# The last layer's down projection with held quadrants, and the modulations beside the first one in column groups

## The chip, the cores and the metric

The kernel runs on one core of a Trainium2 chip. A core has a matrix engine (TensorE, PE in the profile), three engines for elementwise work (VectorE or DVE, ScalarE or ACT, GpSimd or POOL), and a queue engine (SyncE or SP) from which nearly all transfers (DMAs) of this kernel are issued. The engines run side by side, each through its own list of instructions in order, and wait for one another on semaphores. Memory on the core is SBUF (128 partitions) and PSUM, which matmuls write. The metric is the time of one execution on the device, in microseconds; lower is better. Times are the median of several executions; the profile is of one more.

## The reference

One inference step of a two-layer trunk of width 1024 for 1152 tokens: 1024 of a prompt and 8 x 16 of samples. Layer 0 mixes over time with a recurrence (RWKV-7), layer 1 with attention over a band; each is followed by a feed-forward part. All is in float32.

```python
mod = jax.nn.silu(c) @ p['w_ada'][l] + p['b_ada'][l]
sh_m, sc_m, gt_m, sh_f, sc_f, gt_f = jnp.split(mod, 6, axis=-1)
...
x = x + gt_m[:, None, :] * out
h = modulate(rms_norm(x, p['norm_ffn'][l]), sh_f, sc_f)
x = x + gt_f[:, None, :] * swiglu(h, p['w_gate'][l], p['w_up'][l], p['w_down'][l])
```

`c` has one row for the prompt and one for each of the 8 samples, 9 in all; so the *modulations* are a product of 9 rows by a 1024 x 14336 matrix (6144 columns for each layer and 2048 for the shared keys and values). The *down projection* is the product with `w_down`, 2816 x 1024, and the gated addition to x after it.

## The kernel before

**Products.** Feature-major: features lie on partitions, tokens along the free dimension. A float32 operand is split into two parts of a narrower format, hi (ScalarE copies, L276) and lo (VectorE subtracts, L277), and each product is three matmuls, hi x hi, hi x lo and lo x hi (`mm3`). All matmuls go through the helper `mm`, so their line is L143. Tokens are in two groups c: the first with 512, the second with 640.

**The down projection** (`down`, for both layers) takes a Strassen scheme: the output is cut into quadrants (h: upper or lower half of the features, t: first or second half of the tokens of a group), and seven products, the *turns* i = 0, 1, 2, 4, 5, 6, 3, make the four. A turn loads its operand from DRAM in three pieces j per group (`operand`, "h<-bd", L1491) and splits them. For each of four output tiles m of 128 features it loads and splits weights (`weights`, "rq<-ws" or "rq<-in_wd", L1502), runs 11 blocks x 3 matmuls for each group into one PSUM tile ("S" or "PT"), and then evicts (L1555) or adds the result to the accumulator (L1536). One output tile is 66 matmuls, one down projection 28 tiles, 1848 matmuls. In layer 0 the last two turns run once for each group alone. When a quadrant is whole, `result` loads x ("xin<-x", L1529), does the gated addition (`residual`, L1174 to L1179), stores (L1531) and in layer 0 squares the rows for the next norm ("kk", "sqa").

Operands, their raw loads and the accumulator all come from one pool for each group, tag h0 or h1, with 14 slots. The accumulator has four slots for each group (`feats`), held from the first turn to the last; one operand in use has six, hi and lo for three pieces.

**The modulations** are computed in a generator that other loops advance (`step`). Units 12 to 27 of 28 run beside layer 0's down projection, three steps after each output tile (L1570). A unit is 512 outputs. A step loads two tiles of 128 x 512 from `wada` ("aw<-in_wada", L264) and runs four matmuls. Each has 32 stationary columns, the rows of silu(c), and writes its own quarter of PSUM's partitions; the four *column groups* take four different blocks of the contraction. Two steps sum one half of a unit's outputs, so that after four steps (8 blocks) the bank "acc" holds, for each output, four partial sums on four groups of partitions. ScalarE copies the 128 x 512 bank out (L226), and four matmuls with a constant of 16 columns ("acc<-cst,aw") transpose it and sum the quarters; VectorE adds the bias (L232). In the profile a float32 matmul has two records. The aw tiles come from a pool of 11 buffers (tag e) that also serves xin, kk and sqa.

**Order.** The program is traced in Python order, and a planner places each instruction by a simulated time: what is ready first goes first, earlier traced work ahead. So the steps of the modulations end up between matmuls of the products where the planner thinks that their data has come. What it emits is fixed; on the chip each engine takes its list in order.

Of the kernel before, what the change touches and what calls it, by code (L numbers as in the profile page):

```python
# [76 lines left out]
def prep(i):  # L77
    i = {k: np.asarray(v) for k, v in i.items()}
    d = {}
    d["cst"] = _CST  # L80
    d["ti"] = _solver_identity()
    t = np.arange(384)
    rs = np.stack([t % 64 != 0, np.where(t < 256, t % 64, t % 16) != 0]).astype(np.float32)
    d["rs"] = np.ascontiguousarray(np.broadcast_to(rs[:, None], (2, 128, 384)))
    x = np.concatenate([i["x_prompt"][0], i["x_sample"].reshape(128, 1024)], 0)
    d["x"] = np.ascontiguousarray(x.reshape(3, 384, 8, 128).transpose(0, 3, 2, 1))

    xp = np.concatenate([np.zeros((1, 1024), np.float32), i["x_prompt"][0]], 0)
    xg = np.concatenate([xp[16 * g:16 * g + 17] for g in range(64)] + [t for s in i["x_sample"] for t in (s[:1], s)], 0)
    d["xg"] = np.ascontiguousarray(xg.reshape(3, 408, 8, 128).transpose(0, 3, 2, 1))  # L90
    c = np.zeros((32, 1024), np.float32)
    c[0:1] = i["c_prompt"]
    c[1:9] = i["c_sample"]
    d["c"] = np.ascontiguousarray(c.reshape(32, 8, 128).transpose(2, 1, 0))
    wa = np.concatenate([i["w_ada"][0], i["w_ada"][1], i["kv_ada_w"]], 1)
    d["wada"] = np.ascontiguousarray(wa.reshape(2, 4, 128, 28, 2, 256).transpose(3, 4, 0, 2, 1, 5)).reshape(28, 4, 128, 1024)
    par = {f"mix{m}": i["rw_mix"][0, m] for m in range(6)}
    par.update(w0=i["rw_w0"][0], a0=i["rw_a0"][0], kk=i["rw_kk"][0], ka=i["rw_ka"][0], rk=i["rw_rk"][0].reshape(-1),
               lnw=i["rw_lnw"][0], lnb=i["rw_lnb"][0], nm0=i["norm_mix"][0], nm1=i["norm_mix"][1],
               nf0=i["norm_ffn"][0], nf1=i["norm_ffn"][1], kvn=i["kv_norm"],  # L100
               kn=np.tile(i["k_norm"], 16), qn=np.tile(i["q_norm"][0], 16),
               bada=np.concatenate([i["b_ada"][0], i["b_ada"][1], i["kv_ada_b"]]))
# [43 lines left out]
class Trunk:  # L146
# [54 lines left out]
    def ada_steps(self, units, tag="aux", bufs=1, tile=None, sbt=None):  # L201

        nc = self.nc

        def load(u, i):
            w = (tile or self.rawtile)()
            if not isinstance(w, tuple):
                w = w[:, :1024],
            n = 1024 // len(w)
            for j, t in enumerate(w):  # L210
                self.wload(t, self.a["wada"][u, i][:, j * n:(j + 1) * n])
            return [t[:, o:o + 256] for t in w for o in range(0, n, 256)]
        todo = [(u, i) for u in units for i in range(4)]
        ahead = None
        for u in units:
            ps = self.bank(tag, bufs)
            for i in range(4):
                w = ahead or load(*todo.pop(0))
                ahead = load(*todo.pop(0)) if todo and self.fetch_ahead else None
                c = slice(i // 2 * 256, i // 2 * 256 + 256)  # L220
                for q in range(4):
                    mm(nc, ps[32 * q:32 * q + 32, c], self.scT[:, i % 2 * 4 + q, :], w[q], i % 2 == 0, i % 2 == 1)
                if i < 3:
                    yield
            sb = (sbt or tile or self.rawtile)()[:, :512]
            nc.scalar.activation(sb, ps, AF.Copy)  # L226
            for j in range(4):
                mm(nc, ps[:, j * 16:(j + 1) * 16], sb[:, j * 128:(j + 1) * 128], self.C("qs"), True, True)
            pv = ps[:, 0:64].rearrange("p (j n) -> p j n", n=16)[:, :, 0:9]
            bo = PAR["bada"] + u * 4  # L230
            bv = self.par[:, bo:bo + 4].rearrange("p (j o) -> p j o", o=1).broadcast_to([128, 4, 9])
            nc.vector.tensor_tensor(self.mod[:, u * 4:u * 4 + 4, :], pv, bv, ALU.add)  # L232
            yield

    def gain(self, name, sc):

# [1155 lines left out]
    def ffn(self, l, B, W, part1, xsrc, dst, done):  # L1392
# [7 lines left out]
        for f in range(1, 22):  # L1400
            self.gate_up(spill(f), B, self.strassen_weights(l, f, nc.vector if f == 1 else None), (0, 1))
            for g in range(32 * (f - 1) // 21, 32 * f // 21):
                self.down_sums(l, g)
        return self.down(l, xsrc, dst, done)

    def down_open(self, l):

# [55 lines left out]
            gp.tensor_tensor(q[:, 1], q[:, 1], q[:, 0], ALU.subtract)  # L1463
        nc.sync.dma_start(self.Ws[m][:, :, j * 176:(j + 1) * 176], q)

    def down(self, l, xsrc, dst, done):

        nc = self.nc
        gate = 48 * l + 40
        ks = [(j, k) for j, n in enumerate((4, 4, 3)) for k in range(n)]  # L1470
        width = (256, 320)
        part = (slice(0, 256), slice(256, 576))
        turns = [(i, (0, 1)) for i in (0, 1, 2, 4, 5)]
        if l:
            turns += [(i, (0, 1)) for i in (6, 3)]
            self.ada = iter(())
        else:
            turns += [(i, (c,)) for c in (1, 0) for i in (6, 3)]
            part512 = lambda: self.ev("aw")[:, 0:512]
            self.ada = self.ada_steps(range(12, 28), "acc", 1, lambda: (part512(), part512()), part512)  # L1480
        acc, end = {}, iter(())
        sq = [Ctx(), Ctx()]

# [11 lines left out]

        def weights(i, m):
            src = {0: 0, 1: 1, 3: 3}.get(i)
            src = self.Ws[m][:, {5: 0, 2: 1, 6: 2, 4: 3}[i]] if src is None else self.a[f"wd{l}"][:, src, m * 1408:(m + 1) * 1408]
            W = []
            for o, n in ((0, 512), (512, 512), (1024, 384)):  # L1500
                raw = self.halfraw()[:, :n]
# [20 lines left out]
        def result(h, t, m, cs):  # L1522
            f = 4 * h + m
            x = self.ev("xin")[:, 0:576]
            for c in cs:
# [3 lines left out]
                nc.sync.dma_start(x[:, part[c]], xsrc[:, f, at])  # L1529
                self.residual(192 if c * t else n, f, gate, o, x[:, part[c]], o)  # L1530
                nc.sync.dma_start(dst[:, f, at], o)  # L1531
                if l == 0:
                    squares(c, t, f, o)

        def add(o, a, b):
            nc.vector.tensor_tensor(o, a, b, ALU.add)  # L1536

        for i, cs in turns:
            X = operand(i, cs)
            if i == 0:  # L1540
# [2 lines left out]
            for m in range(4):  # L1543
                W = weights(i, m)
                d = self.wide()[:, 256:832]
                for c in cs:
                    for n, (j, k) in enumerate(ks):
                        s = slice(k * 128, (k + 1) * 128)
                        hi, lo = (X[c][j][h][:, k] for h in range(2))
                        self.mm3(d[:, part[c]], W[j][0][:, s], W[j][1][:, s], hi, lo, n == 0, n == 10)  # L1550
                for c in cs:
                    z = d[:, part[c]]
                    c11, c12, c21, c22 = (out(h, t, m, c) for h in range(2) for t in range(2))
# [13 lines left out]
                        add(c21, z, c21)  # L1567
                if i in (1, 5, 6, 3):
                    result(*{1: (0, 0), 5: (0, 1), 6: (1, 1), 3: (1, 0)}[i], m, cs)
                self.step(3)  # L1570
                for _ in range(2):
                    next(end, None)
            if l == 0 and i == 3:
                for g in (self.ada, end):
                    for _ in g:
                        pass
                end = done(cs[0], acc[cs[0]], sq[cs[0]])
        return end

    def dense(self, x2, x3, close):  # L1580
        nc = self.nc
# [530 lines left out]
```

## Time and profile before

| what | us |
|---|---|
| median of three runs | 3791.01 |
| the three runs | 3791.89, 3791.01, 3785.09 |
| the profiled execution, its own time | 3785.41 |
| its span, first to last instruction | 3783.6 |
| first product matmul to end of last, down projection of layer 0 | 1807.3 to 2132.5 |
| the same of layer 1 | 3518.1 to 3778.9 |

The profile's page begins with the busy time of each engine. Other views group instructions by form, list them in order of time, or sum them over given stretches. An idle time is shown with the one who ended it: "[3.45 <-ACT h L276]" means that the engine stood idle for 3.45 us until ScalarE's instruction of line 276 that writes tile h. "SPq" rows are transfers being issued. PEclk is the share of TensorE's clock that was granted.

### The profile page before, as it was taken

The numbers are of one execution on the slowest core, as the hardware profiler recorded it, in microseconds if no ns is written. First come the engines' busy times: TensorE is split into PE (matmuls) and PEld (weight loads), VectorE is DVE, ScalarE is ACT, GpSimd is POOL, SyncE is SP. The second block draws the span as 40 slices with busy tenths as digits, with TensorE's granted clock in tenths as the row PEclk, the third lists the DMA queues.
The fourth block names the chain that finished last, engine by engine and source line by source line (L and its number), as shares of the span: only waits on it lengthen the run. The fifth ranks groups of instructions, "written<-read, shape, count | busy, mean of one in ns | idle before, by whom it ended". The sixth has DMA issues, their size and how long they took to land.

```text
span 3783.6 us, 74619 instructions
## 1 busy us (share of the span) xinstructions
PE 3457.2 (91%) x29078; PEld 3088.6 (82%) x29078; DVE 2248.3 (59%) x4380; ACT 1667.9 (44%) x3182; POOL 769.7 (20%) x743
## 2 busy tenths in 40 slices
PE   5788989999889799999999899789888899999999
PEld 3677768777667699999888879677667799999999
DVE  4666666765446765555446742666575776555555
ACT  4545546554223533333344452556564433333342
POOL 0000000000011066676100000000000156667100
PEclk9887899889689899999999999899999899999999
DMA  5776676677666434445788322445565334444764
GB/s 209 233 220 166 199 217 190 194 202 211 180 186 201 141 127 142 139 138 160 265 319 294 123 73 93 144 143 160 159 205 172 133 123 148 143 139 142 243 205 138
DMA packets 548579, 664.12 MB, mean 176 GB/s; under 512 B 137056, under 2 KB 409440, under 8 KB 543744
## 3 DMA queue, kind: packets, MB, share of 16 engines
q1 hardware_dynamic: 472912, 560.62, 46.7%
q0 software_dynamic: 22224, 80.36, 7.0%
q10 hardware_dynamic: 53088, 18.36, 2.1%
q8 instruction: 229, 3.75, 0.4%
q14 instruction: 126, 1.03, 0.1%
HBM read 482.63 MB, written 176.53 MB: 174 GB/s over the span
## 4 chain that ended last, share of the span: by engine, by line
PE 65%; DMA 13%; DVE 10%; issue 6%; ACT 4%; SPq 1%; POOL 1%; ACTq 0%; DVEq 0%; POOLq 0%
PE S L143 30%; PE PT L143 14%; PE acc L143 12%; PE st L143 3%; PE O L143 2%; DMA raw<-in_rw_o 1%; DVE h L277 1%; PE G L143 1%; PE PT L1937 1%; PE aux L143 1%; DMA TT<-Z 1%; DVE wlo L277 1%; DMA bt<-in_rel 1%; DMA xin<-x 1%; DMA h<-bd 1%
## 5 line engine op out<-in xcount | busy, mean ns | idle before, releaser
L143 PE MATMUL S<-h,w 128*128 128x256 f32 (+1 forms) x7374 | 1036.6, 299 | 23.9 <-ACT h L276 7.4
L143 PEld LDWEIGHTS S<-h,w 128*128 128x128 f32 x7374 | 1002.4, 191 | 46.2 <-issue 19.1
L276 ACT ACTIVATE w<-rq 128x512 fp32r<-128x512 f32 (+1 forms) x500 | 304.4, 614 | 661.4 <-PE S L143 290.0
L277 DVE TENSOR_TENSOR w<-rq,w 128x512 fp32r<-128x512 f32 (+1 forms) x500 | 384.4, 773 | 286.6 <-ACT w L276 247.9
L143 PE MATMUL PT<-h,w 128*128 128x256 f32 (+1 forms) x3714 | 532.0, 298 | 10.2 <-DVE h L277 3.8
L143 PE MATMUL acc<-mx,whi 128*128 128x384 f32 x1728 | 505.9, 370 | 37.2 <-ACT whi L276 15.4
L143 PEld LDWEIGHTS PT<-h,w 128*128 128x128 f32 x3714 | 506.4, 190 | 20.5 <-issue 7.8
L143 PEld LDWEIGHTS acc<-mx,whi 128*128 128x128 f32 x1728 | 335.5, 203 | 67.9 <-ACT whi L276 20.1
L143 PE MATMUL acc<-mx,wlo 128*128 128x384 f32 x864 | 314.9, 365 | 9.0 <-DVE wlo L277 9.0
L1373 POOL TENSOR_TENSOR t<-t,t 128x576 f32<-128x576 f32 (+1 forms) x132 | 221.9, 1682 | 262.9 <-ACT t L1380 154.0
L277 DVE TENSOR_TENSOR h<-h,h 128x1024 fp32r<-128x1024 f32 (+6 forms) x152 | 169.3, 1125 | 121.2 <-ACT h L276 111.2
L276 ACT ACTIVATE h<-h 128x1024 fp32r<-128x1024 f32 (+6 forms) x152 | 142.8, 950 | 147.8 <-DMA h<-bd 110.0
L143 PEld LDWEIGHTS acc<-mx,wlo 128*128 128x128 f32 x864 | 174.1, 202 | 21.6 <-DVE wlo L277 13.9
L277 DVE TENSOR_TENSOR wlo<-raw,whi 128x1024 fp32r<-128x1024 f32 x114 | 139.0, 1221 | 83.6 <-ACT whi L276 82.7
L276 ACT ACTIVATE whi<-raw 128x1024 fp32r<-128x1024 f32 x114 | 119.6, 1053 | 128.7 <-PE acc L143 61.6
L143 PE MATMUL S<-h,wh 128*128 128x320 f32 (+1 forms) x744 | 148.5, 348 | 12.7 <-DVE h L1685 4.7
L143 PE MATMUL acc<-h,wh 128*128 128x256 f32 (+1 forms) x864 | 137.9, 309 | 18.4 <-ACT wh L276 9.1
L1373 DVE TENSOR_TENSOR t<-S,t 128x576 f32<-128x576 f32 (+1 forms) x117 | 86.6, 740 | 113.9 <-PE S L143 113.9
L143 PEld LDWEIGHTS S<-h,wh 128*128 128x128 f32 x744 | 123.4, 195 | 31.3 <-ACT wh L276 6.3
L143 PEld LDWEIGHTS acc<-h,wh 128*128 128x128 f32 x864 | 121.2, 200 | 27.2 <-ACT wh L276 9.8
L1303 POOL TENSOR_TENSOR h<-h,h 128x256 f32<-128x256 f32 x12 | 11.0, 942 | 569.9 <-DMA vf<-in_wo 569.9
L1767 POOL MEMSET qbd<- 128x128 f32 x1 | 0.2, 204 | 560.8 <-PE S L143 560.8
(455 smaller groups left out, 5625.8 us busy)
## 6 DMA issues: line engine op xcount, KB each, us to landing
aw<-in_wada SPq DMA_DIRECT2D x128, 256.0 KB, 5.3
bd<-t SPq DMA_DIRECT2D x154, 160.0 KB, 1.9
rq<-in_wg SPq DMA_DIRECT2D x88, 256.0 KB, 2.9
rq<-in_wu SPq DMA_DIRECT2D x88, 256.0 KB, 2.6
ws<-in_wd SPq DMA_DIRECT2D x64, 352.0 KB, 3.6
ws<-ws SPq DMA_DIRECT2D x64, 352.0 KB, 3.3
bd<-t SPq DMA_DIRECT2D x152, 128.0 KB, 1.8
rq<-ws SPq DMA_DIRECT2D x72, 256.0 KB, 3.4
```

The lines of the kernel that those rows point to most:

```text
L143: return nc.tensor.matmul(out, lhsT, rhs, start=start, stop=stop)
L276: self.nc.scalar.activation(hi, x, AF.Copy)
L277: self.nc.vector.tensor_tensor(lo, x, hi, ALU.subtract)
L1303: gp.tensor_tensor(out[j], x[j], y[j], op)
L1373: return eng.tensor_tensor(out, x, y, ALU.add)
L1767: nc.gpsimd.memset(self.qbd, 0.0)
L1937: nc.tensor.transpose(pt[:, j * 128:(j + 1) * 128], P[:, j * 128:(j + 1) * 128], self.C("ident"))
```

## The change

Layer 0's `down` keeps its accumulator. The modulations beside it come from a new generator, `ada_groups`. Its unit is 1024 outputs (8 units). Each of the four column groups takes 256 outputs of its own and all eight blocks of the contraction, so that nothing is left to be summed over the groups; the weights are laid out anew for it (`wadb`). Two steps (two blocks k, 8 matmuls) are taken together: the two tiles of the first come from the pool with tag e, those of the second from a pool "ws" with two buffers of its own, which earlier stages used for another purpose. The first matmul of the eight reads the tile loaded last; the others are tied behind it on TensorE (`issue_after`). The next loads are traced right after the eight. Once a unit is whole, ScalarE copies 128 x 256, and at the next call two matmuls with a constant of 36 columns (`qg`) transpose it. The generator is advanced after each 44 matmuls of the products, within an output tile, where before it was advanced three times after each tile.

The last layer has its own `down_last`. Instead of a four-slot accumulator it holds the results of turns 0, 2 and 4 in one slot for each group and turn (`T`). Finished quadrants go to a new buffer o of the pool with tag e, which the residual and the store use; both token groups go through one residual.

```diff
+    d["wadb"] = np.ascontiguousarray(wa[:, 6144:].reshape(8, 128, 8, 1024).transpose(2, 0, 1, 3))
+    d["qg"] = np.ascontiguousarray(np.tile(np.eye(32, 9, dtype=np.float32), (4, 4)) * np.repeat(np.repeat(np.eye(4, dtype=np.float32), 32, 0), 9, 1))
...
+    def ada_groups(self, spare):
...
+        qg = self.ev("aw")[:, 0:36]
+        nc.sync.dma_start(qg, self.a["qg"])
+        ev = lambda: self.ev("aw")[:, 0:512]
+        steps = [(u, k) for u in range(8) for k in range(8)]
+
+        def load(n):
+            W = []
+            for (u, k), new in zip(steps[n:n + 2], (ev, spare)):
+                t = [new() for _ in range(2)]
+                for h in range(2):
+                    nc.sync.dma_start(t[h], self.a["wadb"][u, k][:, 512 * h:512 * h + 512])
+                W.append([x[:, o:o + 256] for x in t for o in (0, 256)])
+            return W
+
+        def close(u, sb):
+            ps = self.bank("acc", 1)
+            for j in range(2):
+                mm(nc, ps[:, j * 36:(j + 1) * 36], sb[:, j * 128:(j + 1) * 128], qg, True, True)
...
+            for j in range(2):
+                pv = ps[:, j * 36:(j + 1) * 36].rearrange("p (g n) -> p g n", n=9)
+                nc.vector.tensor_tensor(view(self.mod[:, o:o + 8, :])[:, :, j], pv, bv[:, :, j], ALU.add)
+
+        W, last = load(0), None
+        for n in range(0, 64, 2):
+            if last:
+                close(*last)
+                last = None
+            if steps[n][1] == 0:
+                ps = self.bank("acc", 1)
+            u, k = steps[n]
+            todo = [(k + j, q, W[j][q]) for j in (1, 0) for q in (3, 2, 1, 0)]
+
+            def product(at, q, w):
+                return mm(nc, ps[32 * q:32 * q + 32, 0:256], self.scT[:, at, :], w, at == 1, at == 6)
+            lead = product(*todo.pop(0))
+            with self.tc.issue_after(lead.ins):
+                for x in todo:
+                    product(*x)
+            if k == 6:
+                last = u, ev()[:, 0:256]
+                nc.scalar.activation(last[1], ps[:, 0:256], AF.Copy)
+            if n < 62:
+                W = load(n + 2)
+            yield
+        close(*last)
...
-        if l:
-            turns += [(i, (0, 1)) for i in (6, 3)]
-            self.ada = iter(())
-        else:
-            turns += [(i, (c,)) for c in (1, 0) for i in (6, 3)]
-            part512 = lambda: self.ev("aw")[:, 0:512]
-            self.ada = self.ada_steps(range(12, 28), "acc", 1, lambda: (part512(), part512()), part512)
+        turns += [(i, (c,)) for c in (1, 0) for i in (6, 3)]
+        spare = lambda: self.wq.tile([128, 4, 176], F32, tag="ws", name=self.nm("ws"), bufs=2).rearrange("p a b -> p (a b)")[:, 0:512]
+        self.ada = self.ada_groups(spare)
...
                         self.mm3(d[:, part[c]], W[j][0][:, s], W[j][1][:, s], hi, lo, n == 0, n == 10)
+                        count += 3
+                        if count >= 44:
+                            count -= 44
+                            self.step()
...
-                self.step(3)
...
+    def down_last(self, gate, xsrc, dst):
...
+        def hold(n):
+            T[n] = [self.slot(c)[:, :4 * (256, 320)[c]].rearrange("p (m t) -> p m t", m=4) for c in range(2)]
+
+        def result(h, t, m, o):
...
+            x = self.ev("xin")[:, 0:576]
+            for c in range(2):
+                nc.sync.dma_start(x[:, part[c]], xsrc[:, f, at[c]])
+            self.residual(448 if t else 576, f, gate, o, x, o)
+            for c in range(2):
+                nc.sync.dma_start(dst[:, f, at[c]], o[:, part[c]])
+
+        for i in (0, 1, 2, 4, 5, 6, 3):
+            X = operand(i)
+            if i in (0, 2, 4):
+                hold(i)
...
+                o = None if i in (0, 2, 4) else self.ev("o")[:, 0:576]
...
+                if i in (0, 2, 4):
+                    for c in range(2):
+                        nc.scalar.activation(t[i][c], z[c], AF.Copy)
+                oc = None if o is None else [o[:, part[c]] for c in range(2)]
+                if i == 1:
+                    add(oc, z, t[0])
+                    result(0, 0, m, o)
+                elif i == 4:
+                    add(t[2], t[2], t[4])
+                elif i == 5:
+                    add(t[0], z, t[0])
+                    add(oc, t[2], t[0])
+                    result(0, 1, m, o)
+                elif i == 6:
+                    add(t[0], z, t[0])
+                    add(oc, t[4], t[0])
+                    result(1, 1, m, o)
+                elif i == 3:
+                    add(oc, z, t[0])
+                    result(1, 0, m, o)
```

What `down_last` leaves out here, the loads of operands and weights and the matmuls, is as in `down`.

More of the change, by code (lines that the diff above doesn't have):

```diff
@@ L233, in ada_steps @@
             yield
+    def ada_groups(self, spare):
+        nc = self.nc
+        qg = self.ev("aw")[:, 0:36]
[14 more added lines that the diff above has]
+                mm(nc, ps[:, j * 36:(j + 1) * 36], sb[:, j * 128:(j + 1) * 128], qg, True, True)
+            o = 48 + u * 8
+            bo = PAR["bada"] + o
+            view = lambda t: t.rearrange("p (g j) n -> p g j n", j=2)
+            bv = view(self.par[:, bo:bo + 8].rearrange("p (f o) -> p f o", o=1).broadcast_to([128, 8, 9]))
+            for j in range(2):
[23 more added lines that the diff above has]
+        close(*last)
     def gain(self, name, sc):
@@ L1403, in ffn @@
                 self.down_sums(l, g)
-        return self.down(l, xsrc, dst, done)
+        if l:
+            return self.down_last(48 * l + 40, xsrc, dst)
+        return self.down(48 * l + 40, xsrc, dst, done)
     def down_open(self, l):
@@ L1464, in down_sums, with down @@
         nc.sync.dma_start(self.Ws[m][:, :, j * 176:(j + 1) * 176], q)
-    def down(self, l, xsrc, dst, done):
+    def down(self, gate, xsrc, dst, done):
         nc = self.nc
-        gate = 48 * l + 40
         ks = [(j, k) for j, n in enumerate((4, 4, 3)) for k in range(n)]
@@ L1497, in weights @@
             src = {0: 0, 1: 1, 3: 3}.get(i)
-            src = self.Ws[m][:, {5: 0, 2: 1, 6: 2, 4: 3}[i]] if src is None else self.a[f"wd{l}"][:, src, m * 1408:(m + 1) * 1408]
+            src = self.Ws[m][:, {5: 0, 2: 1, 6: 2, 4: 3}[i]] if src is None else self.a["wd0"][:, src, m * 1408:(m + 1) * 1408]
             W = []
@@ L1531, in result @@
                 nc.sync.dma_start(dst[:, f, at], o)
-                if l == 0:
-                    squares(c, t, f, o)
+                squares(c, t, f, o)
         def add(o, a, b):
             nc.vector.tensor_tensor(o, a, b, ALU.add)
+        count = 0
         for i, cs in turns:
@@ L1569, in down @@
                     result(*{1: (0, 0), 5: (0, 1), 6: (1, 1), 3: (1, 0)}[i], m, cs)
-                self.step(3)
                 for _ in range(2):
                     next(end, None)
-            if l == 0 and i == 3:
+            if i == 3:
                 for g in (self.ada, end):
@@ L1578, in down, with operand, weights, add @@
         return end
+    def down_last(self, gate, xsrc, dst):
+        nc = self.nc
+        ks = [(j, k) for j, n in enumerate((4, 4, 3)) for k in range(n)]
+        part = (slice(0, 256), slice(256, 576))
+        T = {}
+        def operand(i):
+            X = {0: [], 1: []}
+            for c in range(2):
+                n = (256, 320)[c]
+                for j, nk in enumerate((4, 4, 3)):
+                    raw, hi, lo = (self.slot(c, dt)[:, :nk * n].rearrange("p (k t) -> p k t", k=nk) for dt in (F32, F32R, F32R))
+                    nc.sync.dma_start(raw, self.Bd[c][i][j])
+                    self.split(hi, lo, raw)
+                    X[c].append((hi, lo))
+            return X
+        def weights(i, m):
+            src = {0: 0, 1: 1, 3: 3}.get(i)
+            src = self.Ws[m][:, {5: 0, 2: 1, 6: 2, 4: 3}[i]] if src is None else self.a["wd1"][:, src, m * 1408:(m + 1) * 1408]
+            W = []
+            for o, n in ((0, 512), (512, 512), (1024, 384)):
+                raw = self.halfraw()[:, :n]
+                nc.sync.dma_start(raw, src[:, o:o + n])
+                W.append([self.wq.tile([128, 512], F32R, tag="w", name=self.nm("w"), bufs=self.hw[2]) for _ in range(2)])
+                self.split(W[-1][0][:, :n], W[-1][1][:, :n], raw)
+            return W
+        def hold(n):
+            T[n] = [self.slot(c)[:, :4 * (256, 320)[c]].rearrange("p (m t) -> p m t", m=4) for c in range(2)]
+        def result(h, t, m, o):
+            f = 4 * h + m
+            at = [slice(512 * c + (256, 320)[c] * t, 512 * c + (256, 320)[c] * (t + 1)) for c in range(2)]
+            x = self.ev("xin")[:, 0:576]
[8 more added lines that the diff above has]
+                hold(i)
+            for m in range(4):
+                W = weights(i, m)
+                d = self.wide()[:, 256:832]
+                for c in range(2):
+                    for n, (j, k) in enumerate(ks):
+                        s = slice(k * 128, (k + 1) * 128)
+                        hi, lo = (X[c][j][h][:, k] for h in range(2))
+                        self.mm3(d[:, part[c]], W[j][0][:, s], W[j][1][:, s], hi, lo, n == 0, n == 10)
+                z = [d[:, part[c]] for c in range(2)]
+                t = {n: [T[n][c][:, m] for c in range(2)] for n in T}
+                o = None if i in (0, 2, 4) else self.ev("o")[:, 0:576]
+                def add(out, a, b):
+                    for c in range(2):
+                        nc.vector.tensor_tensor(out[c], a[c], b[c], ALU.add)
+                if i in (0, 2, 4):
+                    for c in range(2):
+                        nc.scalar.activation(t[i][c], z[c], AF.Copy)
[16 more added lines that the diff above has]
+                    result(1, 0, m, o)
```

## The prediction

> **What bounds the kernel now.** I read the page first: whose work fills the span.
>
> ```profile
> span 3783.6 us, 74619 instructions
> PE 3457.2 (91%) x29078; PEld 3088.6 (82%) x29078; DVE 2248.3 (59%) x4380; ACT 1667.9 (44%) x3182; POOL 769.7 (20%) x743
> ```
>
> TensorE is busy 91% of the span, so time can be won in two ways: take work from TensorE, or close its gaps. The change touches two stages, the first layer's down projection (about 1807 to 2133 us) and the last layer's (3518 to the end). The view of busy time by stretch shows what they lack; columns are length, then each engine's busy us and count, granted TensorE clock, DMA share, GB/s.
>
> ```profile
> core 0: us, PE busy (x) PEld busy (x) DVE busy (x) ACT busy (x) POOL busy (x), PEclk, DMA share, GB/s
> 1822.00:2088.00 266.00, 263.18 (x2088) 225.89 (x2088) 126.59 (x223) 103.77 (x169) 0.00 (x0) 1.00 0.85 295
> 2103.50:2110.30 6.80, 5.34 (x19) 4.56 (x20) 3.97 (x9) 2.75 (x6) 0.00 (x0) 0.50 0.64 200
> 3554.40:3557.60 3.20, 0.26 (x2) 0.00 (x0) 0.00 (x0) 0.61 (x1) 0.00 (x0) 1.00 0.97 341
> 3557.60:3564.40 6.80, 5.62 (x24) 5.33 (x25) 5.72 (x7) 6.25 (x10) 0.00 (x0) 0.50 0.78 300
> 3600.00:3612.00 12.00, 8.70 (x52) 8.08 (x53) 5.96 (x7) 3.12 (x3) 0.00 (x0) 0.87 0.86 278
> 3612.00:3779.00 167.00, 166.88 (x1246) 166.62 (x1244) 90.96 (x162) 59.65 (x93) 0.00 (x0) 1.00 0.51 162
> ```
>
> The last row is the pace of undisturbed work: 167.00 / 1246 = 0.134 us for a matmul of the products (half have 256 columns, half 320). In the first layer's stage TensorE has no gaps but carries foreign work; in the last layer's it has gaps, each followed by a stretch at half clock. DMA is at 0.85 in the first and has room in the second.
>
> **First layer: the modulation work.** Grouped by form over 1822 to 2088 us (busy us, mean ns, then idle before it and what ended that):
>
> ```profile
> L143 PE MATMUL acc<-aw,scT 128*32 128x256 f32 x512 | 45.6, 387 | 1.7 <-DMA aw<-in_wada 1.6
> L143 PE MATMUL acc<-cst,aw 128*128 128x16 f32 x128 | 15.4, 252 | 0.0
> ```
>
> Each step is 4 matmuls, 8 records, so 512 records are the 64 steps; the 128 of the second row are the 16 units' 4 transposes. How these stand between the products is seen in the timeline (start, length, engine; the next row's start tells when the products go on):
>
> ```profile
> 1826.68 0.63 PE L143 MATMUL acc<-aw,scT 128*32 128x256 f32 x4
> 1827.23 0.70 PE L143 MATMUL S<-h,w 128*128 128x320 f32 x3
> ...
> 1836.16 1.01 SPq L264 DMA_DIRECT2D aw<-in_wada  x2
> 1837.45 0.96 PE L143 MATMUL acc<-cst,aw 128*128 128x16 f32 x8
> 1838.26 3.38 PE L143 MATMUL S<-h,w 128*128 128x256 f32 x22
> 1841.57 1.07 PE L143 MATMUL acc<-aw,scT 128*32 128x256 f32 x16
> 1842.57 2.32 PE L143 MATMUL S<-h,w 128*128 128x320 f32 x14
> ```
>
> Half a step costs 0.55 us (1826.68 to 1827.23), two steps in one run 1.00, a unit's transposes 0.81. [...] The change has 64 steps again, with matmuls of the same size, but in 32 runs of two whole steps, tied together behind one leading matmul that reads the last tile loaded: 32 x 1.07 = 34.2 us against 45.6, saving **11.4**. Transposes go from 16 groups of four to 8 of two: 16 x 0.81 = 13.0 against 8 x 0.41 = 3.2, saving **9.7**; the cost follows the count, since each is the load of a 128x128 operand, and 36 columns instead of 16 are still few. Evictions fall from 16 to 8 on ScalarE and the bias adds stay 16; neither engine is over half busy here, so I cost both at nothing. Bytes and DMA count stay, plus one small load. PE work saved: **21**.
>
> **The new wait.** Of a run's four 256 KB loads, two go to a pool with room for two tiles, so they can be issued only once the run before has read those tiles. Queued behind the leading matmul on TensorE are all later products, and they wait with it. A run is due each 44 product matmuls, 44 x 0.134 = 5.9 us; the two tiles are read first in a run, which gives back about 0.5, so 6.4 us are there. What is needed is two issues, 1.0 us (the SPq row at 1836.16 above), and the landing, in the answer on the tile these loads fill:
>
> ```profile
> DMA to landing us min/median/max: 2.6/5.3/7.9
> ```
>
> At the median 1.0 + 5.3 = 6.3 us: just hidden. At the minimum nothing waits; if all landed at the maximum, 8.9 - 6.4 = 2.5 us, 32 times, 80 us. Before, deeper buffers held such waits to 1.6 us in all (the group's row above). I take the value by the median, a little over its zero: 0.16 us a run, **5 us**; ends 0 and 80. First layer: 21 - 5 = **16**.
>
> After the modulations one more wait stands here, for the squares of the finished rows:
>
> ```profile
> 2104.96 2.50 PE L143 MATMUL S<-sqa,cst 128*128 128x320 f32 x4 [3.48 <-DVE sqa L1520]
> ```
>
> It hangs on a chain of residual loads that the change leaves alone. With the half-clock stretch (2103.50 to 2110.30 above: 15 of its 19 matmuls are products, 2.0 us at full pace, in 5.3 us of busy time) it is worth 3.5 and at most 3.3 more. I leave it in the time; it may go, since the modulations end sooner.
>
> **Last layer: the gaps.** Timeline rows around the first two changes of operand (turns 0 to 1 and 1 to 2; brackets: idle before, and who ended it):
>
> ```profile
> 3528.83 0.69 ACT L1555 ACTIVATE h<-S 128x256 f32<-128x256 f32 x2
> 3545.70 8.95 PE L143 MATMUL S<-h,w 128*128 128x256 f32 x66
> 3546.40 0.70 ACT L1555 ACTIVATE h<-PT 128x256 f32<-128x256 f32 x2
> 3550.70 0.90 SPq L1491 DMA_DIRECT2D h<-bd  x2
> 3556.99 1.06 ACT L276 ACTIVATE h<-h 128x1024 fp32r<-128x1024 f32 x1 [9.89 <-DMA h<-bd]
> 3558.10 0.58 PE L143 MATMUL S<-h,w 128*128 128x256 f32 x1 [3.45 <-ACT h L276]
> 3559.36 2.72 PE L143 MATMUL S<-h,w 128*128 128x256 f32 x11 [0.68 <-DVE h L277]
> ...
> 3588.14 0.82 DVE L1536 TENSOR_TENSOR h<-S,h 128x256 f32<-128x256 f32 x2 [0.35 <-PE S L143]
> 3588.18 0.90 SPq L1491 DMA_DIRECT2D h<-bd  x2
> ...
> 3602.50 1.58 PE L143 MATMUL PT<-h,w 128*128 128x256 f32 x11 [0.53 <-DVE h L277]
> 3607.68 0.39 PE L143 MATMUL PT<-h,w 128*128 128x256 f32 x1 [2.28 <-ACT h L276]
> 3608.67 3.60 PE L143 MATMUL PT<-h,w 128*128 128x256 f32 x14 [0.49 <-DVE h L277]
> ```
>
> The next operand is loaded too late. In turn 1 its first loads (3588.18) go out with the very add of the third output tile (3588.14) that first writes one more slot of the accumulator; in turn 0 they go out soon after the third eviction (3546.40). I read this as the planner giving out the slots of the pool in the order of first use: a load for the next turn queues behind an accumulator slot not yet written. The change holds one slot for a whole quadrant, first written by the first output tile (3528.83 in this trace), and none in turn 1. So turn 1's loads can go out two products, 2 x 8.9 = 17.8 us, earlier, against 3.45 + 0.68 us of lateness; turn 2's too. Also more slots are free: one to three held of 14, not four. The gaps go: 3.45 + 0.68 + 0.53 + 2.28 + 0.49 = 7.4 us. The half clock goes with them: 3557.60 to 3564.40 does 24 x 0.134 = 3.2 us of work in 6.8, and 0.68 of it is counted already, so 2.9; 3600.00 to 3612.00 does 52 x 0.134 = 7.0 in 12, less gaps of 3.3, so 1.7. Together **12.0**. Weights are late next; they are split over one product ahead, so nothing shows.
>
> [...]
>
> What the last layer's change adds: results go to a fresh buffer of the pool that the residual input x is loaded to, and x's load comes after that buffer's first write. It can no longer run far ahead. Inside the stage the 8.9 us of a product hide a load (a landing of about 4 us):
>
> ```profile
> xin<-x SPq DMA_DIRECT2D x32, 160.0 KB, 4.2
> ...
> 3778.92 0.82 DVE L1536 TENSOR_TENSOR h<-S,h 128x256 f32<-128x256 f32 x2 [7.12 <-PE S L143]
> ```
>
> Queued behind the residual on VectorE are weight splits, a product ahead. At the end nothing hides it: between 0 and 4.2 us are added, less the adds' 0.82. The store before it on SP's queue lets it out during the last product, so I take the low side, **1**. Two residuals merged into one save VectorE time that bounds nothing. Last layer: 12 - 1 = **11**.
>
> **Sum.** 16 + 11 = 27 us. The profiled execution took 3785.4 us by its own time (span 3783.6); the three runs have a median of 3791.0 and a lowest of 3785.1. I count from the middle, 3788: **3761 us**.
>
> **Rivals.**
> - *Runs wait for their loads*: landings come later than that median. 0.66 us a run gives back all 21: 3788 - 11 = 3777. For: one pool holds just two tiles, DMA share 0.85, and the same bytes in less time raise it. Against: 1.6 us of waits before.
> - *Slower*: the same wait from 1.0 us a run on (32 saved / 32 runs); at the maximum landing, 80 - 32 = +48: 3836. It needs every landing at its worst, while most waits would relieve the DMA queues.
> - *The last layer's change doesn't do what it says*: the loads stay late for another reason (stores of the last hidden tile, SP's queue): 3788 - 16 = 3772.
> - *The planner places another stage worse*: each new gap of the 3558 us kind costs 3.45 + 0.68 + 2.9 = 7.0; four cancel the gain: 3788. No row speaks for it; the program is reordered as a whole.
>
> **Chances.** Forecast 0.58 (its own range 3749 to 3771); waits eat the first part 0.16; last layer unchanged 0.10; reordering cancels it 0.10; slower 0.06. What a measurement here can tell from no change is 0.2%, 7.6 us: faster means under 3783.4. Faster: 0.58 + 0.10 + 0.14 of the waits' 0.16 = 0.82; within: 0.10 + 0.02 = 0.12; slower 0.06. Range: down to 3744 (no waits, the squares' gap gone, from the lower run level), up to 3787 (half of the reordering case); outside remain slower and the rest of that case.
>
> **What would show it.** Modulation matmuls in runs of 16 records of about 1.07 us, busy near 34; transposes near 4 records at 0.4 us, 8 times; idle before the runs put down to their DMA small. In the last layer the operand loads of turns 1 and 2 a product or more before their turn, no gap over 1 us and no half clock. Wrong if TensorE waits for the modulation loads by more than 0.5 us a run, if the gaps at those operand changes stay, or if the end after the last matmul grows by more than 4 us.

## The result, and the profile after

| | median us | executions | range |
|---|---|---|---|
| before | 3792.56 | 10 | 3785.09 to 3810.40 |
| after | 3776.06 | 10 | 3761.26 to 3783.66 |

The ratio is 0.9949, with a 95% interval of 0.9934 to 0.9964 (it is worked out from the single executions and is not quite the quotient of the two medians). That is 19 us faster, between 14 and 25, against 27 forecast; the median of 3776.06 lies 15 us above the 3761 forecast. The head of the page of the changed kernel, from an execution with a span 10 us shorter than before's:

```profile
span 3773.6 us, 74359 instructions
...
PE 3437.2 (91%) x28982; PEld 3082.6 (82%) x28982; DVE 2247.1 (60%) x4364; ACT 1661.4 (44%) x3174; POOL 770.3 (20%) x743
```

TensorE has 20 us less work (3457.2 before), and the share is again 91%. To see where that went, I cut both traces at the first and the last product of each down projection. First the kernel before (length, busy us and count of each engine, clock, DMA share, GB/s):

```profile
core 0: us, PE busy (x) PEld busy (x) DVE busy (x) ACT busy (x) POOL busy (x), PEclk, DMA share, GB/s
1807.30:2132.50 325.20, 317.74 (x2495) 279.08 (x2494) 174.46 (x312) 133.13 (x223) 9.76 (x9) 0.99 0.81 276
...
3518.10:3778.90 260.80, 252.17 (x1850) 250.37 (x1848) 139.34 (x225) 91.63 (x142) 10.67 (x9) 0.98 0.59 191
```

The same of the kernel after, with one stretch of 10.40 us cut out of the first stage and the end behind the last product:

```profile
1816.30:2142.20 325.90, 300.98 (x2400) 271.69 (x2399) 176.69 (x321) 130.16 (x219) 9.44 (x9) 0.96 0.81 276
...
2102.80:2113.20 10.40, 0.00 (x0) 0.00 (x0) 3.30 (x7) 1.41 (x3) 0.00 (x0) 0.67 0.39 116
...
3521.30:3768.40 247.10, 246.55 (x1849) 246.12 (x1848) 136.48 (x210) 90.25 (x142) 10.24 (x9) 1.00 0.61 201
3768.40:3773.60 5.20, 0.04 (x1) 0.00 (x0) 1.64 (x3) 0.00 (x0) 0.00 (x0) 0.85 0.16 57
```

**Last layer.** 260.80 us became 247.10, at full clock and with 0.55 us idle: 13.7 us won. **First layer.** TensorE is busy 16.8 us less (317.74 to 300.98), and the stage is 0.7 us *longer*. All that was freed stands there as idle time: 325.90 - 300.98 = 24.9 us, where before had 7.5. The groups of this stage after (busy us, mean ns, then idle before it and who ended it) say in front of what:

```profile
L145 PE MATMUL S<-h,w 128*128 128x256 f32 x594 | 80.8, 290 | 4.3 <-ACT h L331 2.6 <-DVE h L332 1.7
...
L145 PE MATMUL PT<-h,w 128*128 128x256 f32 x330 | 47.7, 297 | 5.0 <-ACT wh L331 2.0 <-DVE h L1587 1.7 <-ACT w L331 0.7
L145 PE MATMUL acc<-ws,scT 128*32 128x256 f32 x256 | 20.7, 396 | 3.1 <-DMA ws<-in_wadb 3.1
L145 PE MATMUL acc<-aw,scT 128*32 128x256 f32 x256 | 19.7, 380 | 0.0
L145 PE MATMUL acc<-aw,aw 128*128 128x36 f32 x32 | 4.5, 264 | 1.8 <-ACT aw L284 1.8
L145 PE MATMUL S<-sqa,cst 128*128 128x320 f32 x4 | 2.5, 780 | 10.6 <-DVE sqa L1572 10.6
```

The idle times add up: products 4.3 + 5.0, modulations 3.1, transposes 1.8, squares 10.6, together 24.8. The transposes' matmuls ("acc<-aw,aw") are a quarter in number and 4.5 us busy for 15.4. The largest idle time is the wait for the squares, 3.5 before. In that stretch (the row of 10.40 us above) the DMA engines are at a share of 0.39: TensorE waits, and transfers are not what is scarce there.

The timeline after: a run of modulations; the wait for the squares, with VectorE, ScalarE and SP's queue beside it; a matmul group in the next stage that I use as a mark; the last layer's first operand load for turn 1; and its end:

```profile
1907.35 0.64 PE L145 MATMUL acc<-ws,scT 128*32 128x256 f32 x8
1907.80 0.61 PE L145 MATMUL acc<-aw,scT 128*32 128x256 f32 x8
1908.35 1.45 PE L145 MATMUL S<-h,w 128*128 128x256 f32 x10
...
2105.12 0.55 DVE L1229 SCALAR_TENSOR_TENSOR h<-h,mod,xin 128x320 f32<-128x320 f32 x1 [2.10 <-DMA xin<-x]
2105.70 0.32 SPq L1583 DMA_DIRECT2D x<-h  x1
2105.71 0.47 ACT L1571 ACTIVATE kk<-h 128x320 f32<-128x320 f32 x1 [3.41 <-DVE h L1229]
2106.11 0.38 SPq L1581 DMA_DIRECT2D xin<-x  x1
...
2108.41 0.55 DVE L1229 SCALAR_TENSOR_TENSOR h<-h,mod,xin 128x320 f32<-128x320 f32 x1 [1.71 <-DMA xin<-x]
...
2109.36 0.42 SPq L1581 DMA_DIRECT2D xin<-x  x1
...
2113.31 2.50 PE L145 MATMUL S<-sqa,cst 128*128 128x320 f32 x4 [10.57 <-DVE sqa L1572]
...
2223.12 3.61 PE L145 MATMUL S<-h,wh 128*128 128x512 f32 x15
...
3538.28 0.89 SPq L1648 DMA_DIRECT2D h<-bd  x2
...
3762.39 0.93 SPq L1672 DMA_DIRECT2D xin<-x  x2
```

Read the rows at 2105 to 2109 as a circle: the residual (L1229) waits for x, its store and square follow, then the next x is issued, and 3.3 us later (2105.12 to 2108.41) the next residual can run. TensorE stands at the end of it. The mark, a group of 15 matmuls with 512 columns, came 86.9 us after the first stage's end before (at 2219.35) and comes 80.9 us after it now (2223.12 - 2142.20): the next stage starts more smoothly by 5.9 us. So what these stages account for is 13.7 - 0.5 (the end, 4.7 us before) in the last layer, and 5.9 - 0.7 behind and in the first: 18.4 us, inside the measured interval. The distance between two single spans says less: the first stage begins somewhere between 1804 and 1824 us in the fourteen profiles of this study.

### The profile page after: what moved, and what is told of

It is laid out like the page before. It is cut to its first block, busy times and chain, and to the rows that moved or that the text cites. A ratio compares the mean times of both kernels' runs of the same rounds, so it can differ in the third digit from the quotient of the medians.

```text
span 3773.6 us, 74359 instructions
## 1 busy us (share of the span) xinstructions
PE 3437.2 (91%) x28982; PEld 3082.6 (82%) x28982; DVE 2247.1 (60%) x4364; ACT 1661.4 (44%) x3174; POOL 770.3 (20%) x743
## 4 chain that ended last, share of the span: by engine, by line
PE 65%; DMA 14%; DVE 10%; issue 6%; ACT 4%; SPq 1%; POOL 1%; ACTq 0%; DVEq 0%; POOLq 0%
PE S L145 30%; PE PT L145 15%; PE acc L145 11%; PE st L145 3%; PE O L145 2%; DVE h L332 1%; PE PT L2074 1%; DMA TT<-Z 1%; PE G L145 1%; PE aux L145 1%; DMA h<-bd 1%; DMA raw<-in_rw_o 1%; PE Y L145 1%; DVE wlo L332 1%; DMA Z<-T 1%
## 5 line engine op out<-in xcount | busy, mean ns | idle before, releaser
L145 PE MATMUL PT<-h,w 128*128 128x256 f32 (+1 forms) x3714 | 530.7, 298 | 10.6 <-DVE rq L1428 3.7
L145 PE MATMUL acc<-mx,whi 128*128 128x384 f32 x1728 | 508.3, 372 | 33.7 <-ACT whi L331 12.5
L145 PEld LDWEIGHTS acc<-mx,whi 128*128 128x128 f32 x1728 | 337.7, 204 | 64.1 <-ACT whi L331 16.8
L145 PEld LDWEIGHTS acc<-mx,wlo 128*128 128x128 f32 x864 | 175.4, 203 | 20.8 <-DVE wlo L332 13.2
L2075 ACT ACTIVATE pts<-PT 128x640 f32<-128x640 f32 (+4 forms) x128 | 72.6, 567 | 96.5 <-PE PT L2074 81.5
```

The source lines that it names most:

```text
L145: return nc.tensor.matmul(out, lhsT, rhs, start=start, stop=stop)
L2075: nc.scalar.activation(pts[:, 0:nk * 128], pt[:, 0:nk * 128], AF.Copy)
```

## The experiments

Theory **chain**: the end of the first stage is set by the circle above, so what is taken from TensorE becomes a wait there. Its cause would be the pool with tag e: the planner gives out buffers in the order of first use, each x after the squares' tile kk of the result before, and all behind the modulations' tiles. Rivals: **transfers** (the DMA engines are full), **two-buffer pool** (ws paces the modulations), **late elsewhere** (take one wait away, the next is just behind it).

One table for all runs. Idle is length less PE busy in the first stage; "to the mark" counts from that stage's first product; both, and the last layer, are from the view of stretches and the timeline of each run.

| run | first stage us | idle us | to the mark us | last layer us | ratio to before, 95% |
|---|---|---|---|---|---|
| before | 325.2 | 7.5 | 412.0 | 260.8 | |
| after | 325.9 | 24.9 | 406.8 | 247.1 | 0.9949 [0.9934, 0.9964] |
| e1 last layer only | 323.2 | 6.9 | 409.8 | 247.5 | 0.9960 [0.9945, 0.9976] |
| e2 modulations only | 326.1 | 25.2 | 409.8 | 256.1 | 0.9955 [0.9939, 0.9972] |
| e3 before + early slots | 327.2 | 5.9 | 410.9 | 249.4 | 0.9945 [0.9926, 0.9963] |
| e4 after + early slots | 332.4 | 33.7 | 415.0 | 246.3 | 0.9973 [0.9958, 0.9989] |
| e5 after again | 326.0 | 26.5 | 407.0 | 247.5 | 0.9933 [0.9910, 0.9957] |
| e6 squares over x | 323.0 | 22.5 | 399.2 | 247.4 | 0.9924 [0.9898, 0.9950] |
| e7 four from the deep pool | 323.4 | 20.0 | 408.5 | 246.7 | 0.9925 [0.9901, 0.9949] |
| e8 free x | 316.2 | 17.4 | 391.9 | 246.3 | 0.9915 [0.9890, 0.9940] |
| e9 e8 with old modulations | 326.1 | 11.2 | 400.0 | 247.2 | 0.9926 [0.9908, 0.9944] |
| e10 e8 + early slots | 300.0 | 7.1 | 374.0 | 246.8 | 0.9852 [0.9834, 0.9870] |
| e11 e9 + early slots | 322.9 | 7.8 | 398.3 | 247.3 | 0.9917 [0.9891, 0.9942] |
| e12 e10 again | 299.4 | 6.3 | 373.4 | 247.0 | 0.9866 [0.9841, 0.9891] |

e1 to e4 shared one chip, e5 to e8 a second, e9 and e10 a third, e11 and e12 a fourth. e1 does not touch the code of the first stage, and its profile is 2 us off before there; a difference of that size between two profiles says little.

### The two parts apart: e1 and e2

```diff
+        if l:
+            return self.down_last(48 * l + 40, xsrc, dst)
```

(e1: these lines and `down_last` put into the kernel before; e2: the changed kernel with the old `down` for the last layer.)

> The kernel before with the last layer's part of the change alone. If the gain measured for the whole change (3792.6 to 3776.1, 16.5 us) is the last layer's, as the two traces say (stage 260.8 us to 247.2), this kernel gains 12 to 14 us: about 3779, ratio 0.9964. The prediction's own split (11 of 27) gives 11 us. If the last layer were given back elsewhere and the gain were the first layer's, it gives 0.

> The changed kernel with the last layer's down projection as it was. The prediction's step says 16 us faster than before: 3776, ratio 0.9958. Theory 'the end of the first layer's stage is set by the chain of residual loads and squares, not by TensorE's work' says the freed TensorE time becomes idle in the same stage: 0 to 5 us, ratio 0.9987 to 1.0, with the stage at 325 us as before. Rival 'the two-buffer pool delays the modulations and costs what the steps save' says the same time but a wait of the products on the modulation tiles well over 5 us in the groups.

e1 gives 0.9960, 15 us, and its last layer 247.5 us, as in the changed kernel: the last layer's gain is its own. e2's time and its stage point different ways. The time fell by 11 to 23 us, ratio 0.9955: that is the 16 us of the prediction's step and not the 0 to 5 of the theory. The stage did not get shorter: it is 326.1 us with 25.2 idle, as the chain has it, and the wait for the modulation tiles is 5.6 us in all, not what fills those. The stages account for some 7 us of e2's gain (2.2 to the mark, 4.7 in a last layer whose code is old and whose loads the planner placed a little otherwise); the rest is open, as it is in e3 below, whose stages account for 12.5 of 14 to 28 us. The two parts alone gained 15 and 17 us, together 19: such times hold to some 10 us only, and what follows rests on the stages.

### Early slots: e3 and e4

```diff
                     acc[c] = self.feats(c)
+                    for f in range(0, 8, 2):
+                        nc.gpsimd.memset(acc[c][f][:, 0:1], 0.0)
```

> The kernel before, with one column of each accumulator slot set to zero by GpSimd ahead of the first turn, so that every slot is first written early. Theory 'the planner gives out slots in order of first use, so the next operand's loads queue behind accumulator slots not yet written': the gaps of the last layer at the changes of turns 0 to 1 and 1 to 2 go (7.4 us and 4.6 of half clock), and so do those of the first layer at its turn changes: 12 to 18 us faster, ratio 0.995 to 0.997. Rival 'fewer slots in use is what lets the loads go early': the slots are held longer here, so the gaps stay or grow: ratio 1.000 to 1.003.

> The changed kernel with the same early writes in the first layer's down projection, whose products stall 21.0 us for late operands around the change of turns 1 to 2 and later (10.6 before). If those stalls come from slots first written late, they fall to about 10 and less. Then two cases: if the chain of residual loads and squares sets the stage's end, the wait for the squares grows from 10.6 by as much and the time stays (ratio to the changed kernel 0.999 to 1.0, to before 0.994 to 0.996); if the stalls were on the path, the time falls by 6 to 10 us more, to about 3768, ratio to before 0.9925.

e3 holds the accumulator as long as before, only its slots are first written early, and the last layer drops to 249.4 us. That is 11.4 of the 13.7 us that the new `down_last` brings. So what delayed the loads was the order of first use, as the prediction read it, and not the number of slots held. In the first layer, where the expectation also hoped for a gain, nothing came of it (327.2 us).

e4's groups (idle in the last column):

```profile
L145 PE MATMUL S<-h,w 128*128 128x256 f32 x594 | 80.1, 290 | 0.0
...
L145 PE MATMUL acc<-ws,scT 128*32 128x256 f32 x256 | 21.3, 406 | 9.8 <-DMA ws<-in_wadb 9.7
...
L145 PE MATMUL S<-sqa,cst 128*128 128x320 f32 x4 | 2.5, 781 | 19.5 <-DVE sqa L1572 19.5
```

The products' 4.3 us are gone, and the squares' wait grew from 10.6 to 19.5; the stage is 6.5 us longer, since the modulations also wait more. What is taken from the products goes to the wait for the squares: the chain's mark. That the time would stay was too kind: the mark comes 8.2 us later, and the ratio of 0.9973 lies above both cases. (The products' stalls of 21.0 and 10.6 us in the expectations of e4, e5 and e10 stand in no view by groups; there the products' idle time in this stage is 9.3 us after and 2.3 before.)

### The chain itself: e5 to e8

e5 is the changed kernel once more.

> The changed kernel once more, for a second profile and as the measure for the three runs beside it. If the readings of its first profile are the program's and not one execution's, they come again: last layer's stage 247 us, first layer's stage 326 us with about 21 us of stalls between products and 10 to 11 us of wait for the squares, modulations ending 273 us after the stage's start; ratio to before 0.9935 to 0.9965.

326.0 us, to the mark 407.0, last layer 247.5: the stages come again within 0.4 us, and the squares wait 10.3 us. The ratio, 0.9933, is just below the range expected. e6:

```diff
-        def squares(c, t, f, o):
+        def squares(c, t, f, o, u):
...
-                u = self.ev("kk", 2)[:, :width[c]]
...
-                squares(c, t, f, o)
+                squares(c, t, f, o, x[:, part[c]])
```

> The changed kernel, with the squares of the first layer's results written over the residual input x, whose values are used up by then, in place of a tile of their own. Theory 'chain': a residual load takes its tile after the tile of the squares before it, in the same pool, so load, residual, square and next load follow one another (3.3 us a result, eight of them after the last modulation). Without the squares' tiles the loads go out together: their distance falls well under 3.3 us, the wait for the squares from 10.6 us to 4 or less, and the time by 5 to 9 us against the changed kernel of these runs, if nothing else is late at once. Rival 'transfers': the loads land late because the DMA engines are full (share 0.85): they still arrive every 3 us and the wait stays at 8 or more. Rival 'late elsewhere': the wait goes, but the products after it or the next stage's entry wait for as much: time within 2 us.

Its timeline:

```profile
2088.27 0.37 ACT L284 ACTIVATE aw<-acc 128x256 f32<-128x256 f32 x1
2089.51 2.56 SPq L1580 DMA_DIRECT2D xin<-x  x5
...
2094.40 0.54 DVE L1229 SCALAR_TENSOR_TENSOR h<-h,mod,xin 128x320 f32<-128x320 f32 x1
...
2095.66 0.55 DVE L1229 SCALAR_TENSOR_TENSOR h<-h,mod,xin 128x320 f32<-128x320 f32 x1
...
2096.53 0.55 DVE L1229 SCALAR_TENSOR_TENSOR h<-h,mod,xin 128x320 f32<-128x320 f32 x1
...
2101.65 1.97 PE L145 MATMUL S<-sqa,cst 128*128 128x320 f32 x3 [2.20 <-DVE sqa L1571]
```

Five loads go out as one, residuals follow each other in 0.9 to 1.3 us, not 3.3, and the wait fell to 2.2. The sign given for "transfers", a load every 3 us and a wait of 8 or more, did not come, though the DMA share was 0.77 from 2095.0 to 2099.4 us and 0.91 in the 2.2 us after: "transfers" falls. The loads go out right behind the first write of the last modulation tile (ScalarE's copy at 2088.27), which fits the same queue of first uses, one cause further on; e8 tests it. Products now wait more for adds behind late residuals (7.8 us, 1.7 in the changed kernel), so against e5 the stage won only 3.0 us, and to the mark 7.8: "late elsewhere" holds in part.

e7 takes all four tiles of a run from the deep pool, `self.ada_groups(lambda: self.ev("aw")[:, 0:512])`.

> The changed kernel, with all four tiles of a modulation run from the deep pool, none from the pool with room for two. Theory 'chain': the end of the stage does not hang on that pool: waits of the modulations fall from 3.1 us to under 1, squares still wait 8 us or more, time within 3 us of the changed kernel. Rival 'two-buffer pool': it is what sets the pace of the modulations and so the end of the stage: they end 5 us or more earlier than 273 us after the stage's start, and the time falls by 5 us or more.

The modulations ended 2 us earlier, not 5 (270.8 us after the stage's start, e5 273.1), and the mark came 1.5 us later than in e5: the two-buffer pool did not set the end. Two of the theory's own signs failed as well. The modulations' waits did not fall under 1 us but rose to 7.1, and the squares' matmul had no wait: it had been placed behind products that wait for the same residuals (4.68 us, on VectorE's add). The median time is 5.3 us under e5's, which is what the rival asked for; the mark does not bear it out, and the intervals of the two ratios overlap for the most part. e8 has e7's and e6's edits, and moves x:

```diff
-            x = self.ev("xin")[:, 0:576]
+            x = self.wq.tile([128, 4, 176], F32, tag="ws", name=self.nm("ws"), bufs=2).rearrange("p a b -> p (a b)")[:, 0:576]
```

> Run e7 with e6's edit, and the residual input x of the first layer from the pool with room for two, which only it then uses: its loads queue behind no tile of the modulations. Theory 'chain': squares wait for under 2 us, and as much or more is gained than in e6: 7 to 12 us against the changed kernel, ratio to before 0.9915 to 0.993. Rival 'transfers': as in e6, wait 8 us or more. Rival 'late elsewhere': squares' wait gone, time within 2 us.

No wait for the squares, the stage at 316.2 us, to the mark 15.1 us earlier than e5. The modulations now end 251.3 us after the stage's start. The executions give 11 us between the medians of e5 and e8, and 7 by the two ratios. The stage's other waits are now 8.2 us before modulations and 9.2 before products.

### What the new modulations are worth: e9 to e12

e9 has the old modulations in e8's surroundings; e10 and e11 add e4's memsets to e8 and e9; e12 repeats e10.

> The modulations as before the change, the last layer as after it, and in the first layer e8's free residual input (x from the pool with room for two, squares written over it). What the new modulations are worth where the chain of residual loads does not set the end is the distance from here to e8, whose first stage took 316.2 us. The prediction's step says 16 to 21 us: stage 332 to 337 here, that is, longer than the 323.2 us of the same modulations with the chain, which can't be. Theory 'chain': stage at 318 to 323 us; e8 is faster by 2 to 7 us in the stage and by about 5 at the next stage's entry. Rival 'the chain alone, and the new modulations are worth nothing': stage 316 us and entry as in e8, time as e8 within 2 us.

> e8 with e4's early writes of the accumulator's slots. In e4 they took the stalls between products from 21.0 to 10.9 us, and the wait for the squares grew from 10.8 to 19.9. If the chain is what gave that back, they gain here: stalls between products from 17.8 to 10 or less, first stage from 316.2 us to 308 to 312, time 4 to 8 us under e8 of the runs before, ratio to before 0.989 to 0.991. If the memsets themselves or the later start of the modulations cost (first run 27.2 us after the stage's start in e4, 21.9 without), the stage stays at 316 or grows.

> e9 with the early writes of the accumulator's slots: old modulations, new last layer, free residual input, early slots. Beside e10, which differs in the modulations alone, it shows what the modulation part of the change is worth where neither chain nor late operands set the stage. The prediction's sum of TensorE's work (21 us, with its waits 16) says a first stage of 316 to 321 us against e10's 299.9, and 16 to 21 us of time. If old modulations were held by something else than TensorE's work, the distance comes out below 10 us, as it was between e9 and e8 (326.1 and 316.2).

> e10 once more, beside e11 on the same chip: the first stage at 300 us again, and a ratio to before within 0.9834 to 0.987, if e10's reading is the program's.

e9's 326.1 us fitted no expectation (318 to 323, or 332 and up), but it is 9.9 us longer than e8: with the chain gone the modulations count. With early slots as well they count in full: e10's stage of 300.0 us is shorter than the 308 to 312 expected, and e11's of 322.9 a little longer than its 316 to 321. The stage and groups of e11, old modulations:

```profile
1823.90:2146.80 322.90, 315.08 (x2498) 278.07 (x2496) 180.01 (x332) 135.70 (x228) 9.81 (x17) 0.99 0.82 278
```

```profile
L143 PE MATMUL acc<-aw,scT 128*32 128x256 f32 x512 | 44.3, 390 | 3.1 <-DMA aw<-in_wada 3.1
L143 PE MATMUL acc<-cst,aw 128*128 128x16 f32 x128 | 15.4, 252 | 0.0
```

And of e10, new ones:

```profile
1814.40:2114.40 300.00, 292.90 (x2404) 267.10 (x2403) 179.87 (x335) 130.32 (x222) 9.85 (x17) 0.99 0.87 300
```

```profile
L145 PE MATMUL acc<-aw,scT 128*32 128x256 f32 x512 | 34.3, 385 | 2.3 <-DMA aw<-in_wadb 2.3
L145 PE MATMUL acc<-aw,aw 128*128 128x36 f32 x32 | 4.2, 257 | 0.0
```

22.9 us between two stages that differ in the modulations alone (the new ones here with all tiles from the deep pool), 22.2 of them TensorE's busy time, in both with 7 to 8 us idle. Of 44.3 + 15.4 us 21.2 are gone. e11 and e12, on one chip, differ by 22.6 us in their medians. e10 and e12 beat both kernels: 1.3% to 1.5% under before. e4 shows that the early slots alone are worth less than nothing on the changed kernel, and e8 that the freed chain is worth 15 us to the mark; together they are worth 33.

## Why the prediction was right or wrong

**The time: inside the range, in part by luck.** 3776.06 us lies between the 3744 and 3787 given, but above the forecast's own 3749 to 3771. 4.6 us of the distance to 3761 are the level counted from (3788, measured 3792.56). Of the sum's two terms the last layer's 11 came as 13.2, the first layer's 16 did not come, and 5.9 us came where none were forecast.

**Last layer: right.** 12.0 less 1 was forecast; the stage gave 13.7 and the end took 0.5. The gaps and half clock went together (granted 0.98 before, 1.00 after). The cause given, slots handed out by first use, is shown by e3. Turn 1's loads go out 17.0 us after the stage's start (3538.28), before 32.6. The late load of x costs as little as said: it is issued during the last product (3762.39).

**TensorE's work: right.** A run of two steps takes 1.00 us (1907.35 to 1908.35) for 1.07 forecast, and e10 has 34.3 us for 34.2. 21 us saved were forecast, e11 to e10 has 21.2 in the groups. In the changed kernel itself 16.8 show; around its new waits part of the stage ran at half clock (0.50 from 1912.5 to 1918.5 and from 2108 to 2116 us; 0.96 granted in the stage for 0.99), and there the same matmuls take longer (11 of 256 columns 2.71 us from 1912.98, at full clock 10 of them 1.45 us from 1908.35), which fits the difference.

**The new wait: right in size.** 3.1 us for the ws tiles, against 5, but in a single wait and not a little in each run; 1.8 us before transposes were not forecast. The rival of runs that wait for their loads named almost the measured time (3777) by a mechanism that did not take place.

**The step that failed** is the one behind the new wait: "It hangs on a chain of residual loads that the change leaves alone. ... I leave it in the time". The 16 us were subtracted from the stage as if TensorE set its end, while the last wait of the stage, by that very sentence, was for a chain on other engines. Such a wait is no fixed sum; here it took up what was freed ahead of it. The runs put 0.7 us longer in place of 16 us shorter. The trace of before had the circle already:

```profile
2099.51 0.55 DVE L1174 SCALAR_TENSOR_TENSOR h<-h,mod,xin 128x320 f32<-128x320 f32 x1 [0.76 <-DMA xin<-x]
...
2100.50 0.38 SPq L1529 DMA_DIRECT2D xin<-x  x1
...
2103.32 0.55 DVE L1174 SCALAR_TENSOR_TENSOR h<-h,mod,xin 128x320 f32<-128x320 f32 x1 [1.13 <-DMA xin<-x]
...
2104.28 0.42 SPq L1529 DMA_DIRECT2D xin<-x  x1
```

Loads of a tile that has a pool of 11 buffers, 3.8 us apart and each behind the residual before it: that pattern points to a buffer that was waited for, not to a transfer. The squares' matmul came 297.7 us after the stage's first product before, and comes 297.0 after. The prediction also hoped that this wait "may go, since the modulations end sooner". They did not: their last matmul starts 273.0 us after the stage's first product (2089.3), before 273.9 (2081.2). Both times the squares follow 24 us behind it (the rows show the groups in which they stand):

```profile
2081.00 0.62 PE L143 MATMUL acc<-aw,scT 128*32 128x256 f32 x4
2104.96 2.50 PE L143 MATMUL S<-sqa,cst 128*128 128x320 f32 x4 [3.48 <-DVE sqa L1520]
```

```profile
2089.08 0.61 PE L145 MATMUL acc<-aw,scT 128*32 128x256 f32 x8
2113.31 2.50 PE L145 MATMUL S<-sqa,cst 128*128 128x320 f32 x4 [10.57 <-DVE sqa L1572]
```

This tells where the saved time went. Up to the last modulation matmul TensorE does 1514 matmuls of the products before and 1588 after, 74 more or 9.9 us at 0.134, and stands idle 9.9 us for 3.8. Those products are then missing from the 24 us that the residual loads behind the modulations take, and the squares' wait grows. It was the shared pool that tied both ends: with x out of it the last modulation matmul comes after 1412 products and 251.3 us (e8), with early slots after 233.7 us (e10), and with the old modulations after 255.7 (e9). The edits of e6 and e7 alone, which leave x in that pool, have it after 277.5 and 270.8 us.

**What made up for it** was not forecast: 5.9 us at the entry of the next stage. With the chain freed it is more (e9, old modulations, 73.9 us from the end to the mark, for 86.9), which suggests, but does not show, that the residuals that run on past the end are part of it; why the change alone already won there was not tried apart.

## What to carry to other kernels

Before work is subtracted from a busy engine, look at its last wait in that stage: if another chain ends there, even a short wait (3.5 us here) can grow by what is freed ahead of it, and the stage stays as long until that chain is shortened. Where a planner gives out one pool's buffers in the order of first use, a tile that is written late holds back the loads traced behind it; give loads that should run ahead a tag of their own, or touch the slots early. And free both chain and operands before judging either: alone they gave 15 us to the mark and a loss of 8 here, together 33.

## What the runs showed of the hardware

The four matmuls of the squares took 2.50 us behind the wait of 10.57, and 1.24 in e10, where they did not wait. The granted clock was 0.67 on average over the 10.40 us without a product and 0.71 over the 5.80 us behind them. In steps of 2 us from 2102 on it was 1.00, 1.00 and 0.58, then 0.50 up to 2116, 0.86 and again 1.00. It was lower around shorter gaps too: 0.86 over 23.7 us from 1908.3 in the changed kernel, where the longest idle time was 1.93 us, and 0.50 there from 1912.5 to 1918.5.

New was how far single executions stand apart. From the fourteen profiles the start of the first stage, 1804.2 to 1823.9 us, has a spread as large as the whole gain, with no edit ahead of it, while the same stage of the same kernel came again within 0.6 us (e10 and e12, after and e5). Stages can be compared between two profiles, spans hardly.
